# Two of four weight pieces of the sparse attention's compression in buffers outside the weight ring, and the keys of two branches in one tile

## Chip, cores and metric

The kernel runs on one core of a Trainium2 chip. The metric is the device time of one execution in microseconds; a time of the kernel is the median of its runs. Three runs of the kernel before took 1446.93, 1449.24 and 1449.49 us, so its time is 1449.24 us.

## What is computed

A decoder trunk of two layers on 512 tokens of width 1024, in float32. Each layer projects the normed input `h` through one matrix `w_in`, whose columns feed three token mixers that run side by side; their outputs are joined, projected through `w_out`, and a SwiGLU feed-forward block follows. The change lies in mixers A and B:

```python
h = rms_norm(x, norm_mix) * (1 + sc_m) + sh_m
(aq, ak, av, bq, bkc, bvc, bks, bvs, bkw, bvw, bg, cqkv, cz, ca, cb) = jnp.split(h @ w_in, points, axis=-1)
o_a = banded_attention(apply_rope(aq), apply_rope(ak), av, A_WINDOW, attn_sinks)
o_b = nsa_mixer(bq, bkc, bvc, bks, bvs, bkw, bvw, bg, ...)   # compressed, selected and window branches
o_c = gated_delta_net(cqkv, ca, cb, cz, ...)
x = x + gt_m * (jnp.concatenate([o_a, o_b, o_c], axis=-1) @ w_out)

def compress_tokens(x, w1, w2, pe):        # once for bkc, once for bvc
    win = concatenate([strides[:, :-1], strides[:, 1:]], axis=2) + pe   # 31 blocks of 32 tokens, stride 16
    return silu(win.reshape(31, 32 * 64) @ w1) @ w2                      # w1: 2048 x 256
```

## The kernel before, in words

Everything lies in SBUF, features on the 128 partitions. A projection of 128 columns of `w_in` takes a float32 weight piece, splits it into a high part `whi` (ScalarE, line 584) and a low part `wlo` (VectorE as a rule, line 585), and multiplies each of 8 slices in three matmuls of 128x512 (`product`, lines 588 to 595): 24 matmuls into a PSUM tile `pj`. The tiles `pj` of mixers A and B come from two PSUM banks in turn, so the third of them waits until the first has been read.

Weights come by DMA, all issued by one in-order queue, SP's. Each takes the next buffer of the **weight ring**, `wraw`: two buffers of 128x2048 floats (1 MB). An issue waits until the last reader of the buffer's former content is done: the split of a projection's piece, or the compression's matmuls.

Beside the ring there are buffers of 128x1024 floats, `ab0` to `ab3`. Through `ab0`, `ab1` and `ab2` goes in turn a side job of layer 0, `araw` (lines 385 to 445): pieces of the modulation weights `ada_w`, which ScalarE and GpSimd, at the end VectorE (line 416), sum up, and whose sum TensorE transposes (`pada`, line 438). Afterwards `aq` (queries of A), `bq` and `bqr` (queries of B, plain and rotated) live there.

The stage of the change is in `layer`, lines 987 to 1099, in this order:

- `single` on columns BKC, the inputs of the compression; `shifted` copies them into `kvx`;
- `single` on `raw2`, a second ring piece of 128 columns: the selected branch's keys (copied from the piece before, line 1063) and the window branch's keys (line 1064); `rope` rotates them into `ksw`;
- `squeeze(0)`; `single` on AK (line 1068), a ring piece of its own with the keys of mixer A, `rope_k`; `squeeze(1)`;
- `pair(AQ, rope_q)`: two projections with `squeeze(2)` and `squeeze(3)` behind them;
- the rest of the compression (`pct`, `pkc`, `pvc`), then `pair(BQ, both)`.

`squeeze(piece)` (lines 1044 to 1058) loads a quarter of the two compression weights `w1` as one ring tile `craw` (two DMAs of 512 KB), adds the position code to windows of `kvx` (`xw`, VectorE) and issues 8 small matmuls (32x256 results) into `pcmp`. The trace counts each float32 matmul of `pcmp`, `pi`, `psc`, `pt` twice.

A scheduler puts the recorded instructions of each engine into their final order; priorities (`prio`) shift some. So this stage is woven together with mixer C: a 64x64 inverse, whose first part is a ladder of 30 GpSimd operations (lines 844 to 848); VectorE takes its result at lines 850 to 853 (`td`), TensorE at 859 and 868 (`pi`), and so on to lines 893 to 906; then the recurrence over 4 chunks (`pvn`, `pks`, ...). Behind it come the attention blocks (`psc` scores, maxima `mx` at line 1133, softmax, `poa`, `pob`).

Of the kernel before, what the change touches and what calls it, by code (L numbers as in the profile page):

```python
# [8 lines left out]
F32 = mybir.dt.float32  # L9
# [9 lines left out]
NK = 8  # L19
# [23 lines left out]
 'cz0': 0,  # L43
 'czp': 0,
 'do': 1,
 'dtI': 'G',
 'e0': 'GGGV',
 'sv': 0,
# [126 lines left out]
  'wt': ['ab0', 'ab3', 'ab2', 'kvx']},  # L175
 {}]
KS[3].update({'sv': 4, 'ld': 1})
KN = {}


# [50 lines left out]
def trunk(ctx, tc, I, out, dbg=None):  # L231
    stage(0)
    nc = tc.nc
# [36 lines left out]
    AB3 = ("ab0", "ab1", "ab2")  # L270
    turns = {}

    def AB(name, shape=(128, 1024), dt=F32, tag=None, tags=AB3):
        if tag is None:
            turns[tags] = turns.get(tags, -1) + 1
            tag = tags[turns[tags] % len(tags)]
        pool = c8 if tag == "kvx" else ab
        t = pool.tile([128, 1024], dt, tag=tag, name=name)
        return t.rearrange("p (a b) -> p a b", a=shape[1]) if len(shape) == 3 else t
# [290 lines left out]
    def raw_piece(w, r0, nk, c0, n):  # L570
        raw = wr.tile([128, 2048], F32, tag="wraw", name="wraw")
        v = raw[:, :nk * n].rearrange("p (k c) -> p k c", k=nk)
        nc.sync.dma_start(v, w[r0:r0 + 128 * nk, c0:c0 + n].rearrange("(k p) c -> p k c", p=128))
        return v
# [54 lines left out]
    def layer(l, side, norm, vt):  # L629
# [100 lines left out]
        def pair(c0, then, first=None):  # L730
            raw = raw_piece(w_in, 0, NK, c0, 256) if first is None else first
            for j in range(2):
                to = j and first is not None and KN["sp"] >> l & 1
                to = [AB("wsp", (128, 8, 128), F32R, q) for q in ("ab3", "kvx")] if to else None
                with behind(l == 0 and c0 == CQKV + 768 and KN["ga"] & 1):
                    w = split(raw[:, :, j * 128:j * 128 + 128], to, E[KN["w0"]] if l == 0 and first is not None else V)
                p = P("mm" if first is None else "gd" if l else KN["cp"], "pj")
                for sl in HALF[2:] if first is None or (l == 0 and KN['fh']) else HALF[:2]:
                    product(p, w, h, 0, sl)
                then(p, j)  # L740
                with behind(l == 0 and first is not None and KN["ga"] & 2):
                    feed()
# [244 lines left out]
        def rope(p, dst):  # L987
            with prio("rope"):
                w = S2("sw")
                for r in range(4):  # L990
                    cpy(KN['ros'], w[32 * r:32 * r + 32], p[32 * (r ^ 1):32 * (r ^ 1) + 32])
                V.tensor_tensor(dst, p, const("cos"), op=OP.mult)
                E[KN["roM"]].tensor_tensor(w, w, const("sin"), op=OP.mult)
                V.tensor_add(dst, dst, w)
# [12 lines left out]
                for b in (slice(0, 64), slice(64, 128)):  # L1007
                    V.tensor_tensor(lo[b], src[a], hi[a].bitcast(F32), op=OP.subtract)

        aq, bq, bqr = (AB(n, (128, 2, 512), tag=t) for n, t in zip(("aq", "bq", "bqr"), AB3))  # L1010
        kvx = AB("kvx", (128, 2, 512), tag="kvx")
        ksw = c8.tile([128, 512], F32, tag="ksw", name="ksw")
        akd = AB("akd", (128, 2, 512), tag="ab3")
# [1 line left out]
        def single(view, then):  # L1015
            w = split(view)
            p = P("mm", "pj")
            product(p, w, h)
            then(p)
# [23 lines left out]

        def squeeze(piece):
            with prio("sq"):
                raw = wr.tile([128, 2, 4, 256], F32, tag="wraw", name="craw")
                for j, n in ((0, "cmp_k_w1"), (1, "cmp_v_w1")):
                    nc.sync.dma_start(raw[:, j], I[n][l, 512 * piece:512 * piece + 512].rearrange("(i p) c -> p i c", p=128))
                xw = xws[piece % 2]
                for j in range(2):  # L1050
                    win = bass.AP(tensor=kvx.tensor, offset=kvx.offset + 512 * j + 8 * piece,
                                  ap=[kvx.ap[0], [2, 4], [16, NCMP]])
                    V.tensor_tensor(xw[:, j, :, 0:NCMP], win,
                                    pet[:, 16 * j + 4 * piece:16 * j + 4 * piece + 4].unsqueeze(2).to_broadcast([128, 4, NCMP]),
                                    op=OP.add)
                    for i in range(4):
                        T.matmul(pc[32 * i:32 * i + 32, 256 * j:256 * j + 256], xw[:, j, i], raw[:, j, i],
                                 start=(piece == 0 and j == 0), stop=(piece == 3 and j == 1), tile_position=(0, 32 * i))

        raw = raw_piece(w_in, 0, NK, BKC, 256)  # L1060
        single(raw[:, :, 0:128], shifted)
        raw2 = wr.tile([128, 2048], F32, tag="wraw", name="wraw")[:, :1024].rearrange("p (k c) -> p k c", k=8)
        V.tensor_copy(raw2[:, :, 0:64], raw[:, :, 128:192])
        nc.sync.dma_start(raw2[:, :, 64:128], w_in[:, BKW:BKW + 64].rearrange("(k p) c -> p k c", p=128))
        single(raw2, lambda p: rope(p, ksw))

        squeeze(0)
        single(raw_piece(w_in, 0, NK, AK, 128), rope_k)
        squeeze(1)

        def rope_q(p, j):
# [23 lines left out]
        for hd in range(NH):  # L1095
            V.tensor_copy(vcb[32 * hd:32 * hd + NCMP, hd // 2, 64 * (hd % 2):64 * (hd % 2) + 64],
                          p[32 * hd:32 * hd + NCMP, 0:64])

        pair(BQ, both)
        if KN["czp"] == 2:  # L1100
            czs()
# [445 lines left out]
```

## Time and profile before

| | us |
|---|---|
| median of three runs | 1449.24 |
| profiled execution, its own time | 1450.83 |
| its span, first to last instruction | 1449.1 |
| TensorE busy | 1363.4 (94%) |
| VectorE busy | 975.1 (67%) |
| ScalarE busy | 685.9 (47%) |
| GpSimd busy | 496.9 (34%) |
| mean granted TensorE clock | 0.968 of 2.4 GHz |

Busy time of TensorE is modelled and does not mean full rate. The granted clock of a stretch is 1.00 at 2.4 GHz and 0.50 at 1.2 GHz. Of an idle time the profile names what ended it. Layer 0 reaches the stage of the change at about 185 us, layer 1 at about 890 us.

### The profile page before, as it was taken

What the parts mean: (1) busy time and instruction counts of PE and PEld (TensorE: products, weight loads), DVE (VectorE), ACT (ScalarE), POOL (GpSimd) and SP (SyncE); (2) the same over time, 40 slices, a digit from 0 to 9 for tenths busy, and PEclk for the clock granted to TensorE, in tenths of its full rate; (3) what the DMA queues carried; (4) which work ended last, traced back from release to release, by engine and by line L of the source; (5) the groups of instructions that cost most, each with busy time, mean ns of one, the idle gap of its engine ahead of it and who ended that gap; (6) DMA issues with size and microseconds to landing.
All of it is one profiled execution on the core that took longest, in us unless ns stands there. A gap on an engine that the chain in (4) does not pass through costs nothing.

```text
span 1449.1 us, 22839 instructions
## 1 busy us (share of the span) xinstructions
PE 1363.4 (94%) x8925; PEld 1166.2 (80%) x8925; DVE 975.1 (67%) x1773; ACT 685.9 (47%) x1250; POOL 496.9 (34%) x402
## 2 busy tenths in 40 slices
PE   3889988999999999999999999989989999999997
PEld 2667866877887888788898888667879999898997
DVE  6766886885646555456456667589647787777775
ACT  4576635574543432342245462568544444353441
POOL 4446541254432320140033013224335444253330
PEclk7799999799999999999999999989999999999999
DMA  9647453002147564555441123400130323323322
GB/s 325 208 159 231 142 173 124 29 2 88 30 146 244 162 204 140 166 174 174 133 146 34 59 88 103 153 30 2 43 104 16 121 97 99 106 94 110 117 88 74
DMA packets 137169, 171.57 MB, mean 118 GB/s; under 512 B 14779, under 2 KB 95333, under 8 KB 136933
## 3 DMA queue, kind: packets, MB, share of 16 engines
q1 hardware_dynamic: 137060, 170.11, 36.3%
q8 instruction: 70, 1.15, 0.3%
q14 instruction: 39, 0.31, 0.1%
HBM read 168.00 MB, written 2.10 MB: 117 GB/s over the span
## 4 chain that ended last, share of the span: by engine, by line
PE 66%; DVE 12%; DMA 7%; ACT 5%; POOL 4%; issue 4%; SPq 0%; POOLq 0%; DVEq 0%; ACTq 0%
PE pd L301 16%; PE pm L301 10%; PE pj L301 7%; PE pg L301 7%; PE pu L301 7%; DMA araw<-in_ada_w_dram 5%; PE pw L301 3%; PE psc L301 2%; DVE wlo L585 2%; POOL araw L421 2%; PE pwc L301 2%; PE ppt L1111 2%; PE pob L301 1%; PE pvt L301 1%; DVE araw L416 1%
## 5 line engine op out<-in xcount | busy, mean ns | idle before, releaser
L584 ACT ACTIVATE whi<-wraw 128x1024 fp32r<-128x1024 f32 (+1 forms) x181 | 179.3, 993 | 303.0 <-PE pd L301 99.2
L585 DVE TENSOR_TENSOR wlo<-wraw,whi 128x1024 fp32r<-128x1024 f32 (+1 forms) x171 | 218.5, 1279 | 107.1 <-ACT whi L584 104.9
L301 PE MATMUL pj<-hh,whi 128*128 128x512 f32 (+1 forms) x376 | 149.8, 400 | 7.1 <-DVE cacc L719 3.6
L301 PE MATMUL pj<-hl,whi 128*128 128x512 f32 (+1 forms) x376 | 147.9, 394 | 1.0 <-DVE hl L500 1.0
L301 PE MATMUL pj<-hh,wlo 128*128 128x512 f32 (+1 forms) x376 | 148.0, 394 | 0.8 <-DVE wlo L585 0.8
L421 POOL TENSOR_TENSOR araw<-araw 128x512 f32<-128x512 f32 x55 | 76.7, 1394 | 164.0 <-DMA araw<-in_ada_w_dram 62.8
L599 DVE SCALAR_TENSOR_TENSOR x<-pd,mods,x 128x512 f32<-128x512 f32 (+1 forms) x112 | 73.3, 671 | 65.2 <-PE pd L301 64.0
L301 PE MATMUL pd<-fl,whi 128*128 128x512 f32 x288 | 112.2, 390 | 0.0
L301 PE MATMUL pd<-fh,whi 128*128 128x512 f32 x288 | 111.1, 390 | 1.2 <-ACT whi L584 1.2
L301 PE MATMUL pd<-fh,wlo 128*128 128x512 f32 x288 | 107.3, 390 | 0.0
L301 PE MATMUL pm<-tmix,whi 128*128 128x256 f32 x576 | 102.8, 283 | 0.0
L301 PEld LDWEIGHTS pj<-hh,whi 128*128 128x128 f32 x376 | 72.6, 194 | 24.8 <-issue 5.5
L301 PEld LDWEIGHTS pm<-tmix,whi 128*128 128x128 f32 x576 | 88.2, 192 | 0.0
L301 PEld LDWEIGHTS pj<-hh,wlo 128*128 128x128 f32 x376 | 72.8, 194 | 16.6 <-DVE wlo L585 2.1
L301 PEld LDWEIGHTS pj<-hl,whi 128*128 128x128 f32 x376 | 73.1, 194 | 14.6 <-DVE hl L500 1.2
L301 PE MATMUL pg<-hh,whi 128*128 128x512 f32 (+1 forms) x208 | 78.2, 376 | 3.9 <-ACT hh L496 2.1
L301 PE MATMUL pg<-hh,wlo 128*128 128x512 f32 (+1 forms) x208 | 78.6, 378 | 2.2 <-DVE wlo L585 2.2
L301 PE MATMUL pu<-hh,wlo 128*128 128x512 f32 (+1 forms) x208 | 78.7, 378 | 1.8 <-DVE wlo L585 1.8
L421 POOL TENSOR_TENSOR araw<-araw,araw 128x512 f32<-128x512 f32 x36 | 51.3, 1426 | 81.5 <-ACT araw L420 80.3
L420 ACT ACTIVATE araw<-araw,scol 128x512 f32<-128x512 f32 x91 | 60.6, 715 | 39.1 <-DMA araw<-in_ada_w_dram 37.9
L301 PE MATMUL pg<-hl,whi 128*128 128x512 f32 (+1 forms) x208 | 78.0, 375 | 0.6 <-DVE hl L500 0.6
L301 PE MATMUL pu<-hl,whi 128*128 128x512 f32 (+1 forms) x208 | 77.9, 375 | 0.0
(383 smaller groups left out, 3646.0 us busy)
## 6 DMA issues: line engine op xcount, KB each, us to landing
wraw<-in_w_gate_up_dram SPq DMA_DIRECT2D x44, 1024.0 KB, 5.3
araw<-in_ada_w_dram SPq DMA_DIRECT2D x80, 512.0 KB, 3.9
wraw<-in_w_in_dram SPq DMA_DIRECT2D x22, 1024.0 KB, 5.1
wraw<-in_w_down_dram SPq DMA_DIRECT2D x20, 1024.0 KB, 5.3
araw<-in_ada_w_dram SPq DMA_DIRECT2D x8, 1024.0 KB, 8.3
wraw<-in_w_out_dram SPq DMA_DIRECT2D x8, 1024.0 KB, 5.1
craw<-in_cmp_k_w_dram SPq DMA_DIRECT2D x8, 512.0 KB, 4.0
craw<-in_cmp_v_w_dram SPq DMA_DIRECT2D x8, 512.0 KB, 4.9
```

The lines of the kernel that those rows point to most:

```text
L301: return T.matmul(o, l, r, start=start, stop=stop)
L416: V.scalar_tensor_tensor(o, t, scol[:, k:k + 1], acc, op0=OP.mult, op1=OP.add)
L420: A.activation(t, t, AF.Copy, scale=scol[:, k:k + 1])
L421: G.tensor_tensor(o, t, acc, op=OP.add)
L584: A.activation(hi, src, AF.Copy)
L585: eng.tensor_tensor(lo, src, hi.bitcast(F32), op=OP.subtract)
L599: V.scalar_tensor_tensor(xt[m][:, sl], p[:, sl], g, xt[m][:, sl], op0=OP.mult, op1=OP.add)
L1111: T.transpose(p[:, (o + kb) * 128:(o + kb) * 128 + 128], pt[:, kb * 128:kb * 128 + 128], ident)
```

## The change

Two edits. `squeeze` for pieces 0 and 2 (table entry `cab`) takes the buffers `ab1` (weights of the keys) and `ab2` (weights of the values) instead of a ring tile; pieces 1 and 3 stay in the ring. For that `bq` and `bqr`, which take the same buffers, are now named only ahead of `pair(BQ, both)`. And the columns AK are loaded into the unused half of the ring tile `raw2`, right behind the window keys, instead of into a ring tile of their own. The number of DMAs, their bytes and all arithmetic are the same.

```diff
--- before.py
+++ after.py
@@ -43,6 +43,7 @@
  'cz0': 0,
  'czp': 0,
  'do': 1,
+ 'cab': (0, 2),
  'dtI': 'G',
  'e0': 'GGGV',
  'sv': 0,
@@ -1007,7 +1009,7 @@
                 for b in (slice(0, 64), slice(64, 128)):
                     V.tensor_tensor(lo[b], src[a], hi[a].bitcast(F32), op=OP.subtract)
 
-        aq, bq, bqr = (AB(n, (128, 2, 512), tag=t) for n, t in zip(("aq", "bq", "bqr"), AB3))
+        aq = AB("aq", (128, 2, 512), tag="ab0")
         kvx = AB("kvx", (128, 2, 512), tag="kvx")
         ksw = c8.tile([128, 512], F32, tag="ksw", name="ksw")
         akd = AB("akd", (128, 2, 512), tag="ab3")
@@ -1043,9 +1045,13 @@
 
         def squeeze(piece):
             with prio("sq"):
-                raw = wr.tile([128, 2, 4, 256], F32, tag="wraw", name="craw")
+                if piece in KN["cab"]:
+                    raw = [AB("craw", tag=t).rearrange("p (a b) -> p a b", a=4) for t in AB3[1:]]
+                else:
+                    t = wr.tile([128, 2, 4, 256], F32, tag="wraw", name="craw")
+                    raw = [t[:, 0], t[:, 1]]
                 for j, n in ((0, "cmp_k_w1"), (1, "cmp_v_w1")):
-                    nc.sync.dma_start(raw[:, j], I[n][l, 512 * piece:512 * piece + 512].rearrange("(i p) c -> p i c", p=128))
+                    nc.sync.dma_start(raw[j], I[n][l, 512 * piece:512 * piece + 512].rearrange("(i p) c -> p i c", p=128))
                 xw = xws[piece % 2]
                 for j in range(2):
                     win = bass.AP(tensor=kvx.tensor, offset=kvx.offset + 512 * j + 8 * piece,
@@ -1054,18 +1060,19 @@
                                     pet[:, 16 * j + 4 * piece:16 * j + 4 * piece + 4].unsqueeze(2).to_broadcast([128, 4, NCMP]),
                                     op=OP.add)
                     for i in range(4):
-                        T.matmul(pc[32 * i:32 * i + 32, 256 * j:256 * j + 256], xw[:, j, i], raw[:, j, i],
+                        T.matmul(pc[32 * i:32 * i + 32, 256 * j:256 * j + 256], xw[:, j, i], raw[j][:, i],
                                  start=(piece == 0 and j == 0), stop=(piece == 3 and j == 1), tile_position=(0, 32 * i))
 
         raw = raw_piece(w_in, 0, NK, BKC, 256)
         single(raw[:, :, 0:128], shifted)
-        raw2 = wr.tile([128, 2048], F32, tag="wraw", name="wraw")[:, :1024].rearrange("p (k c) -> p k c", k=8)
+        raw2 = wr.tile([128, 2048], F32, tag="wraw", name="wraw").rearrange("p (k c) -> p k c", k=8)
         V.tensor_copy(raw2[:, :, 0:64], raw[:, :, 128:192])
         nc.sync.dma_start(raw2[:, :, 64:128], w_in[:, BKW:BKW + 64].rearrange("(k p) c -> p k c", p=128))
-        single(raw2, lambda p: rope(p, ksw))
+        nc.sync.dma_start(raw2[:, :, 128:256], w_in[:, AK:AK + 128].rearrange("(k p) c -> p k c", p=128))
+        single(raw2[:, :, 0:128], lambda p: rope(p, ksw))
 
         squeeze(0)
-        single(raw_piece(w_in, 0, NK, AK, 128), rope_k)
+        single(raw2[:, :, 128:256], rope_k)
         squeeze(1)
 
         def rope_q(p, j):
@@ -1096,6 +1103,7 @@
             V.tensor_copy(vcb[32 * hd:32 * hd + NCMP, hd // 2, 64 * (hd % 2):64 * (hd % 2) + 64],
                           p[32 * hd:32 * hd + NCMP, 0:64])
 
+        bq, bqr = (AB(n, (128, 2, 512), tag=t) for n, t in zip(("bq", "bqr"), AB3[1:]))
         pair(BQ, both)
         if KN["czp"] == 2:
             czs()
```

The scheduler orders the changed program anew. In the changed kernel the line numbers are higher, by 2 up to line 1043 of before and by 6 to 8 behind it (859 is 861, 1057 is 1063, 1133 is 1141).

SP's queue in layer 0, from the load of the window keys on (rows of 128x8x128 are AK, of 128x8x256 the two query tiles of A). Before:
```order
L1064 DMA wraw<-in_w_in_dram 128x8x64
L399 DMA araw_1306<-in_ada_w_dram 128x2x512
L399 DMA araw_1362<-in_ada_w_dram 128x2x512
L399 DMA araw_1366<-in_ada_w_dram 128x2x512
L1048 DMA craw<-in_cmp_k_w_dram 128x4x256
L1048 DMA craw<-in_cmp_v_w_dram 128x4x256
L399 DMA araw_1417<-in_ada_w_dram 128x2x512
L573 DMA wraw<-in_w_in_dram 128x8x128
L399 DMA araw_1413<-in_ada_w_dram 128x2x512
L1048 DMA craw<-in_cmp_k_w_dram 128x4x256
L1048 DMA craw<-in_cmp_v_w_dram 128x4x256
L573 DMA wraw<-in_w_in_dram 128x8x256
```
and in the changed kernel:
```order
L1070 DMA wraw<-in_w_in_dram 128x8x64
L401 DMA araw_1306<-in_ada_w_dram 128x2x512
L1071 DMA wraw<-in_w_in_dram 128x8x128
L401 DMA araw_1362<-in_ada_w_dram 128x2x512
L401 DMA araw_1366<-in_ada_w_dram 128x2x512
L1054 DMA craw<-in_cmp_k_w_dram 128x4x256
L1054 DMA craw<-in_cmp_v_w_dram 128x4x256
L401 DMA araw_1417<-in_ada_w_dram 128x2x512
L401 DMA araw_1413<-in_ada_w_dram 128x2x512
L1054 DMA craw<-in_cmp_v_w_dram 128x4x256
L575 DMA wraw<-in_w_in_dram 128x8x256
L1054 DMA craw<-in_cmp_k_w_dram 128x4x256 x2
```
AK is no longer behind two compression loads; what follows is piece 1 of the compression, then the value half of piece 0 and at once the queries of A. Before, these stood behind pieces 0 and 1.

VectorE in layer 0, behind the last sum of the side job (`kr`: keys of A being rotated; `lane`: the ladder's result, first step of the inverse on this engine; `wlo`: splits of the two query tiles of A). Before:
```order
L994 TENSOR_TENSOR ksw<-ksw,sw 128x512
L1053 TENSOR_TENSOR xw_102<-kvx,pet 128x4x31
L439 TENSOR_REDUCE mods_90<-pada 128x4
L1053 TENSOR_TENSOR xw_102<-kvx,pet 128x4x31
L440 TENSOR_TENSOR mods_90<-mods_90,vcol_88 128x4
L1053 TENSOR_TENSOR xw_103<-kvx,pet 128x4x31 x2
L992 TENSOR_TENSOR kr<-pj,cst 128x512
L993 TENSOR_TENSOR sw<-sw,cst 128x512
L585 TENSOR_TENSOR wlo<-wraw,whi 128x1024
L994 TENSOR_TENSOR kr<-kr,sw 128x512
L585 TENSOR_TENSOR wlo<-wraw,whi 128x1024
L850 TENSOR_SCALAR lane<-lane,cst 128x256 x2
```
and in the changed kernel:
```order
L995 TENSOR_TENSOR sw<-sw,cst 128x512
L587 TENSOR_TENSOR wlo<-wraw,whi 128x1024
L729 TENSOR_TENSOR cv<-pt,sg 128x4x128
L996 TENSOR_TENSOR ksw<-ksw,sw 128x512
L441 TENSOR_REDUCE mods_90<-pada 128x4
L442 TENSOR_TENSOR mods_90<-mods_90,vcol_88 128x4
L587 TENSOR_TENSOR wlo<-wraw,whi 128x1024
L994 TENSOR_TENSOR kr<-pj,cst 128x512
L995 TENSOR_TENSOR sw<-sw,cst 128x512
L996 TENSOR_TENSOR kr<-kr,sw 128x512
L1059 TENSOR_TENSOR xw_102<-kvx,pet 128x4x31 x2
L852 TENSOR_SCALAR lane<-lane,cst 128x256 x2
```
The two splits of the queries of A moved from right ahead of the ladder's result (`lane`) to ahead of the rotation of the keys of A.

TensorE in layer 0 at the first product of the inverse, `pi` of line 859 (861). Before:
```order
L301 MATMUL pj<-hh_278,whi 128x512
L301 MATMUL pj<-hl_279,whi 128x512
L301 MATMUL pj<-hh_278,wlo 128x512
L1057 MATMUL pcmp<-craw,xw_102 32x256
L859 MATMUL pi_1640<-td,at 32x32 x64
L1057 MATMUL pcmp<-craw,xw_102 32x256 x3
L301 MATMUL pj<-hh_276,wlo 128x512
```
and in the changed kernel:
```order
L303 MATMUL pj<-hl_279,whi 128x512
L303 MATMUL pj<-hh_278,wlo 128x512
L303 MATMUL pj<-hh_278,whi 128x512
L861 MATMUL pi_1640<-td,at 32x32 x64
L1063 MATMUL pcmp<-craw,xw_102 32x256 x8
L303 MATMUL pj<-hl_279,whi 128x512
L303 MATMUL pj<-hh_278,wlo 128x512
```
Between the last transposes of `cacc`, at 198.9 us in the trace, and this product there are 40 matmuls of `pj` and 21 of `pcmp` before, and 60 of `pj` and 16 of `pcmp` in the changed kernel.

## Rows read from the trace of the kernel before

**Rows 1.** Page, part 1: busy time of TensorE, its share, instructions.
```profile
PE 1363.4 (94%) x8925; PEld 1166.2 (80%) x8925; DVE 975.1 (67%) x1773; ACT 685.9 (47%) x1250; POOL 496.9 (34%) x402
```

**Rows 2.** Windows, layer 0: length, busy time of PE, PEld, DVE, ACT, POOL; clock, DMA share, GB/s.
```profile
203.20:207.00 3.80, 3.80 (x12) 2.97 (x11) 3.80 (x8) 0.00 (x0) 3.46 (x5) 0.55 0.68 214
...
213.90:217.10 3.20, 3.20 (x12) 2.55 (x9) 1.61 (x2) 2.51 (x4) 2.75 (x6) 0.50 0.25 16
...
253.60:268.00 14.40, 14.38 (x91) 11.71 (x92) 10.39 (x29) 4.88 (x13) 1.19 (x2) 0.50 0.19 71
```

**Rows 3.** Waits of TensorE, 190 to 270 us: total, times, longest, us.
```profile
PE psc L301 <- DVE mx L1133: 5.7, 1, 5.7
PE pj L301 <- ACT whi L584: 2.6, 1, 2.6
PE pada L438 <- DVE araw L416: 1.6, 1, 1.6
PE pcmp L1057 <- DMA craw<-in_cmp_k_w_dram: 0.7, 1, 0.7
```

**Rows 4.** Timeline of TensorE, layer 0: start, length (us), line, operation, tiles, count, wait before.
```profile
199.41 1.06 PE L1057 MATMUL pcmp<-craw,xw 128*32 128x256 f32 x12
...
204.40 0.63 PE L301 MATMUL pj<-hl,whi 128*128 128x512 f32 x1
...
206.11 0.63 PE L301 MATMUL pj<-hh,wlo 128*128 128x512 f32 x1
...
208.24 1.07 PE L1057 MATMUL pcmp<-craw,xw 128*32 128x256 f32 x16
...
221.67 1.29 PE L859 MATMUL pi<-td,at 32*32 32x32 f32 x128
...
223.78 0.39 PE L301 MATMUL pj<-hh,whi 128*128 128x512 f32 x1
...
228.34 0.39 PE L301 MATMUL pj<-hh,wlo 128*128 128x512 f32 x1
...
247.41 0.48 PE L301 MATMUL psc<-akd,aq 64*128 64x128 f32 x2
```

**Rows 5.** Timeline of SP's queue, layer 0: DMA issues.
```profile
196.90 0.37 SPq L1048 DMA_DIRECT2D craw<-in_cmp_k_w_dram  x1
...
203.33 0.37 SPq L573 DMA_DIRECT2D wraw<-in_w_in_dram  x1
...
223.57 0.37 SPq L573 DMA_DIRECT2D wraw<-in_w_in_dram  x1
```

**Rows 6.** Page, part 6: issues, KB each, median us to landing.
```profile
wraw<-in_w_in_dram SPq DMA_DIRECT2D x22, 1024.0 KB, 5.1
```

**Rows 7.** Timeline of ScalarE, layer 0.
```profile
228.78 2.00 ACT L584 ACTIVATE whi<-wraw 128x1024 fp32r<-128x1024 f32 x2 [5.17 <-DMA wraw<-in_w_in_dram]
...
240.78 2.39 ACT L305 ACTIVATE sw<-pj 32x512 f32<-32x512 f32 x4
```

**Rows 8.** Timeline of VectorE, layer 0.
```profile
195.66 1.21 DVE L585 TENSOR_TENSOR wlo<-wraw,whi 128x1024 fp32r<-128x1024 f32 x1
...
201.00 1.03 DVE L416 SCALAR_TENSOR_TENSOR araw<-araw,scol 128x512 f32<-128x512 f32 x1
...
217.67 0.61 DVE L850 TENSOR_SCALAR lane<-lane,cst 128x256 f32<-128x256 f32 x2 [2.17 <-POOL lane L848]
218.32 1.18 DVE L852 STREAM_TRANSPOSE td<-lane 128x512 f32<-128x512 f32 x1
```

**Rows 9.** Timeline of TensorE, layer 1.
```profile
909.47 0.50 PE L301 MATMUL pj<-hh,wlo 128*128 128x512 f32 x1 [0.52 <-DVE wlo L585]
...
916.04 0.50 PE L301 MATMUL pj<-hh,whi 128*128 128x512 f32 x1 [0.72 <-DVE kr L992]
```

**Rows 10.** Timeline of VectorE, layer 1.
```profile
914.77 0.61 DVE L850 TENSOR_SCALAR lane<-lane,cst 128x256 f32<-128x256 f32 x2 [3.86 <-POOL lane L848]
915.30 0.68 DVE L992 TENSOR_TENSOR kr<-pj,cst 128x512 f32<-128x512 f32 x1
```

## Prediction

> **What bounds the kernel.** Three views, in this order. The page first: TensorE is busy for 1363.4 us [rows 1] of a span of 1449.1, so a change in one stage is worth what TensorE idles there, and what it loses at the low clock. Then the waits of TensorE around the stage [rows 3]: 1.6 us for the side job's last sum, 2.6 for the split of the first query tile of A, 0.7 for a compression load, together 4.9; and, after the last projection, 5.7 for the maxima of the scores. Then the windows behind them [rows 2]: 3.8 us at 0.55 and 3.2 us at 0.50 of the clock. At half rate half the time is lost, so 1.7 + 1.6 = 3.3 us. The stage itself wastes 4.9 + 3.3 = 8.2 us in layer 0, and after the wait for scores 14.4 us pass at 0.50.
>
> SP's queue tells why. The queries of A are issued at 203.33, behind both compression pieces, when the matmuls of piece 0 have given back a ring buffer [rows 5]. A load of this kind lands after 5.1 us [rows 6], so at 208.4. TensorE has then just finished the keys of A: at 208.24 it turns to compression matmuls [rows 4], and then it has nothing.
>
> **The change, step by step, layer 0.** The ring has to pass six pieces in this stage instead of nine; bytes and matmuls stay the same.
>
> *The load of the queries.* Its buffer is now `raw2`, free when the keys of A are split: 195.66 + 1.21 = 196.9 [rows 8]. Ahead of it on SP stands only the value half of piece 0, whose buffer a VectorE sum ahead of that split frees. So it is issued 6.4 us earlier and lands at 202.0. Behind it on SP wait the key half of piece 0 (free only with `pada`, 202.7), then pieces 3 and 2; the key half lands about 5 us later, by 208, and is needed at 210. On VectorE the two splits of the queries now stand ahead of the key rotation, two cheap copies for the modulation and the ladder's result. If they had to wait for the load, these would wait too; with the load at 202.0 and 1.0 us for the high part, the input is there at 203.0, and they run at once.
>
> *TensorE up to the first product of the inverse.* Twenty projection matmuls take 223.78 to 228.34, so 0.228 us each; eight of `pcmp` take 1.0 [rows 4]. The new order has 60 projections (13.7 us), 16 `pcmp` (2.0) and the transposes of `pada` (0.6) from 199.41 on. Two waits remain: `pada` comes up at 201.3 and its sum ends at 201.00 + 1.03 [rows 8], so 0.7; the low part of a tile is late by 0.5, as now in layer 1 [rows 9]. With 0.3 for changes between tiles TensorE arrives at 217.2. But the product needs `td`, and line 850 starts at 217.67 only because the GpSimd ladder ends then; line 852 ends at 218.32 + 1.18 = 219.5 [rows 8], one small window addition now in between makes it 219.9. Nothing ahead of the ladder is changed. So **a new wait of 2.7 us** stands here, and the product starts at 219.9 instead of 221.67 [rows 4]. That is 1.8 us earlier, and with 20 projections more (4.6) and 5 `pcmp` less (0.6) behind it: 5.8 us ahead.
>
> *The clock.* The waits of 1.6 and 2.6 us were each followed by the low clock, the 0.7 alone cannot be told apart [rows 2, 3]. I charge the new wait with 1.6, the smaller of the two losses: 4.2 us ahead. The Trainium skill (TensorE: Matmul & The Clock Gate, "What's actually happening") calls the half rate the default state and says that activity releases it. The two stretches agree: they end while dense projections run. What that rule would do where thin work follows the wait is a rival below; by it the gain would be gone.
>
> A second count, by waits alone: removed 8.2; new 0.7 + 0.5 + 2.7 + 1.6 = 5.5; gain 2.7. The two differ by gaps too small to be named as waits. I take the first, which goes by places, and keep 2.7 as the lower bound.
>
> *The scores behind the stage.* They wait for VectorE's queue, which starts with the rotation of B's first query tile; ScalarE begins that at 240.78 [rows 7]. In the new order this tile has moved up: 219.9 + 1.2 for the product + 2.0 for 16 `pcmp` + 2.5 for 11 projections + 1.2 for the second product + 1.0 for `pct` + 3.4 for 15 projections + 1.6 for the clock = 232.8, and 1.6 for a split and a copy ahead of the rotation: 234.4, 6.4 us earlier. So VectorE gains 6.4 where TensorE gains 4.2, and the wait of 5.7 shrinks by up to 2.2. This asks for the load of B's queries in time. It waits for the matmuls of piece 1, about 212, behind piece 2: with 5.1 us for each, 222.4, needed at 223.6. Now it is issued at 223.57, and the split waits 5.17 for it [rows 5, 7]. I take 5.3, between 4.2 and 6.4.
>
> *Layer 1.* Waits of 0.52 and 0.72 [rows 9]. The second is for the bank that the key rotation reads (line 992, at 915.30), and this stands on VectorE behind the ladder's result (914.77) in both orders [rows 10]. TensorE comes earlier to the same gate and waits longer. Bounds: a gain of 1.2 when both waits really go; a loss of 1.6 when the gathered wait lowers the clock as in layer 0. I take a loss of 0.5, nearer to the second, since the gate does not move.
>
> *The rest.* In both attentions the same instructions are woven in another order. No row prices that. I take 0 and allow 2.6 either way, the longest wait seen inside the stage. Loading piece 0 of layer 1 much earlier, and the wider stride of the split's source, cost nothing that TensorE waits for.
>
> **Sum.** 5.3 - 0.5 = 4.8 us. The profiled execution took 1450.83, so 1446.0; the median of the three runs is 1.6 lower, so **1444.4 us**.
>
> **The rivals.**
>
> *Given back (same).* The ladder is the real bound: TensorE gains 1.8 at the product, and the changed order of the attention and the clock take the rest. For it: the ladder does not move, and in layer 1 it gates already. Against it: behind the product the load of B's queries is early as well. By the lower bound of 2.7 less the 0.5 and a further 0.7: 1.5 us, 1447.7.
>
> *Clock (slower).* The two gathered waits, 2.7 us in layer 0 and about 2 in layer 1, are followed by the thin work of the inverse and `pcmp`, not by dense projections. Where little ran, after the 5.7 wait, the clock stayed at 0.50 for 14.4 us [rows 2]. At the low clock a projection takes (206.11 - 204.40) / 4 = 0.43 [rows 4], 0.2 more. I have charged 8 of them. With 32 the gain of 4.8 is gone; it is slower by over 0.2% from 46 on, and with 50 it gives 1444.4 + 8.4 = 1452.8. Against it: in the present order thin work stands at the same places, without a wait ahead of it, and the low clock ended after 3 to 4 us.
>
> *Much faster.* The waits go as worked out, the clock does not fall at the product, and the wait of 5.7 with half of its 14.4 us at low clock shrinks further: about 4 more, 1440.
>
> *The load stays late.* If the queries of A landed at 208.4 as now, TensorE would idle 5 us from 204 on and reach the product at about 222: no change, 1449. It speaks against this that nothing on SP ahead of that load waits for longer than 196.9; its chance is in that of the first rival.
>
> **How the numbers follow.** About 0.2%, 2.9 us, can be told from no change. Forecast 0.56; given back, with the late load, 0.22; much faster 0.10; clock 0.12. The forecast with its own bounds reaches from 1441.5 to 1447; all but 0.02 of it lies below 1446.3. So faster 0.54 + 0.10 = 0.64, same 0.02 + 0.22 = 0.24, slower 0.12. The range takes in the given-back case with its 2.6 us of attention, leaves out most of the clock case and the far end of the much faster one: 1438.5 to 1451.
>
> **What would show it.** In the changed kernel's profile: the issue of the queries of A at about 197 and no wait of TensorE for their high part; one wait of 2 to 3 us ahead of the first `pi`, which starts at about 220; low clock for some 3 us behind it; B's query rotation on ScalarE at 234 to 235; the scores' wait near 3.5 us. In layer 1 the first `pi` at an unchanged distance from the ladder. I am wrong if the queries' load is still issued after 200, if `pi` starts after 221.5, or if the windows behind it show the low clock for over 8 us.

## Result, and the profile of the changed kernel

Seven runs of the changed kernel took 1436.08 to 1443.84 us, median 1439.41; seven of the kernel before 1446.93 to 1453.24, median 1449.24. The ratio is 0.9942, 95% interval 0.9925 to 0.9959: 8.4 us faster, between 5.9 and 10.9 (the two medians lie 9.8 apart). A second measurement (run e5 below) gave 0.9946 (0.9925 to 0.9968). The prediction was 1444.4, range 1438.5 to 1451: the right side, inside the range but close to its lower end, and 5 us too high (3.6 by the ratio).

The profiled execution of the changed kernel took 1443.84 us. It was already 2.35 us ahead when layer 0's stage began, with the same instructions up to there: the last transposes of `cacc` start at 196.54 and not at 198.89. To compare places in layer 0 with before, add 2.35 to its times.

The page, part 1, answers to [rows 1]:

```profile
PE 1361.6 (94%) x8925; PEld 1167.6 (81%) x8925; DVE 968.1 (67%) x1773; ACT 687.5 (48%) x1250; POOL 496.8 (34%) x402
```

TensorE is busy for 1.8 us less (before: 1363.4) in a span that is 7.1 us shorter: most of what went is idle time. The waits of TensorE, 188 to 268 us, answer to [rows 3]:

```profile
PE psc L303 <- DVE mx L1141: 3.8, 2, 3.2
PE pi L861 <- DVE td L854: 2.2, 1, 2.2
PE pada L440 <- DVE araw L418: 0.8, 1, 0.8
PE pj L303 <- DVE wlo L587: 0.8, 1, 0.8
```

The wait of 2.6 for the high part of A's queries and the 0.7 for a compression load are gone, the one for the side job is 0.8 instead of 1.6, the one for the scores 3.2 instead of 5.7. New are 2.2 for `td`, the ladder's result, and 0.8 for a low part. The waits inside the stage thus sum to 3.8 us, before to 4.9: by waits alone the stage has won little. SP's queue in layer 0, against [rows 5] (first row the queries of A, last row those of B, between them the compression):

```profile
194.56 0.37 SPq L575 DMA_DIRECT2D wraw<-in_w_in_dram  x1
200.46 6.28 SPq L1054 DMA_DIRECT2D craw<-in_cmp_k_w_dram  x2
...
210.26 0.37 SPq L575 DMA_DIRECT2D wraw<-in_w_in_dram  x1
```

The queries of A are issued at 194.56 + 2.35 = 196.9 (before: 203.33), those of B at 212.6 (223.57). ScalarE, against [rows 7]: the first split of B's queries and the rotation of B's first tile:

```profile
219.25 1.06 ACT L586 ACTIVATE whi<-wraw 128x1024 fp32r<-128x1024 f32 x1 [5.58 <-DMA wraw<-in_w_in_dram]
...
232.43 1.79 ACT L307 ACTIVATE sw<-pj 32x512 f32<-32x512 f32 x3
```

VectorE takes the ladder's result, against [rows 8]:

```profile
215.59 0.62 DVE L852 TENSOR_SCALAR lane<-lane,cst 128x256 f32<-128x256 f32 x2 [5.83 <-POOL lane L850]
...
216.39 1.05 DVE L854 STREAM_TRANSPOSE td<-lane 128x512 f32<-128x512 f32 x1
```

TensorE at the first product, at the first scores and at the end of the longest wait for their maxima, against [rows 4]:

```profile
217.59 1.44 PE L861 MATMUL pi<-td,at 32*32 32x32 f32 x128 [2.19 <-DVE td L854]
...
239.19 0.48 PE L303 MATMUL psc<-akd,aq 64*128 64x128 f32 x2
...
245.08 0.58 PE L303 MATMUL psc<-akd,aq 64*128 64x128 f32 x1 [3.20 <-DVE mx L1141]
```

Before, that wait ended here:

```profile
253.59 0.79 PE L301 MATMUL psc<-akd,aq 64*128 64x128 f32 x2 [5.70 <-DVE mx L1133]
```

The product starts 4.08 us earlier than before, 1.73 without the offset; the scores 8.22, or 5.87; the wait ends 8.51 earlier, or 6.16. The first scores are a little flattered: 92 small `pi` products of the inverse (as the trace counts them), which stood ahead of them, now stand behind them, where TensorE waits anyway. The windows of the two stretches at the low clock, and of the one behind the product in layer 1 (columns as in [rows 2]):

```profile
217.60:222.00 4.40, 4.40 (x150) 2.42 (x151) 4.20 (x7) 1.34 (x2) 0.42 (x1) 0.61 0.03 10
242.40:259.40 17.00, 14.31 (x91) 12.09 (x92) 14.03 (x39) 8.25 (x23) 2.34 (x3) 0.50 0.17 63
910.50:915.00 4.50, 3.70 (x133) 3.33 (x134) 1.82 (x3) 3.20 (x6) 0.51 (x1) 0.62 0.02 4
```

**Where the time went.** Six instructions with the same operands in every kernel bound four stretches of TensorE's queue: in each layer the stage (from the last `pt<-cst,cacc`) and the attention (up to the first matmul `pg` or `pu` of the feed-forward block). The stage ends at the first `psc` in layer 0 and at the last `pj` in layer 1. So the wait for the first maxima, 5.7 us before, counts to the attention of layer 0. For layer 1, before:

```profile
900.40 0.38 PE L726 MATMUL pt<-cst,cacc 128*128 128x128 f32 x2
...
943.53 0.39 PE L301 MATMUL pj<-hh,wlo 128*128 128x512 f32 x1
...
1083.04 0.39 PE L301 MATMUL pg<-hh,whi 128*128 128x256 f32 x1 [2.11 <-ACT hh L496]
```

and after:

```profile
894.16 0.38 PE L728 MATMUL pt<-cst,cacc 128*128 128x128 f32 x2
...
937.99 0.40 PE L303 MATMUL pj<-hh,wlo 128*128 128x512 f32 x1
...
1074.78 0.39 PE L303 MATMUL pg<-hh,whi 128*128 128x256 f32 x1 [2.09 <-ACT hh L498]
```

So the stage of layer 1 is 0.70 longer (43.83 against 43.13) and its attention 2.72 shorter (136.79 against 139.51). In layer 0 the stage is 5.87 shorter, the attention 1.25. Together -9.14; with the offset of -2.35, +3.23 in the feed-forward block of layer 0, whose instructions are the same in almost the same order, and +1.33 behind layer 1's attention, that makes the 6.9 us by which TensorE ends earlier in this execution. The 3.23 is not the change's: the repeat of the same kernel (e5) has -0.32 there. It is the clock, which was at half rate at the start of that block in this execution, so 3.4 us lost, and not in e5:

```profile
378.92:385.75 6.83, 6.44 (x31) 6.35 (x31) 3.91 (x9) 3.08 (x8) 3.98 (x5) 0.50 0.02 4
```
```profile
374.20:385.00 10.80, 9.86 (x79) 9.60 (x80) 9.87 (x22) 7.95 (x20) 5.72 (x8) 1.00 0.01 2
```

### The profile page after: what moved, and what is told of

Its sections match the earlier page's. It is cut to its first block, busy times and chain, and to the rows that moved or that the text cites. A ratio compares the mean times of both kernels' runs of the same rounds, so it can differ in the third digit from the quotient of the medians.

```text
span 1442.0 us, 22848 instructions
## 1 busy us (share of the span) xinstructions
PE 1361.6 (94%) x8925; PEld 1167.6 (81%) x8925; DVE 968.1 (67%) x1773; ACT 687.5 (48%) x1250; POOL 496.8 (34%) x402
## 4 chain that ended last, share of the span: by engine, by line
PE 65%; DVE 12%; DMA 8%; POOL 6%; issue 4%; ACT 4%; SPq 0%; POOLq 0%; DVEq 0%; ACTq 0%
PE pd L303 15%; PE pm L303 10%; PE pu L303 7%; PE pg L303 7%; DMA araw<-in_ada_w_dram 7%; PE pj L303 6%; POOL araw L423 3%; PE pwc L303 3%; PE pw L303 3%; DVE wlo L587 2%; PE psc L303 2%; PE pob L303 2%; PE ppt L1119 2%; DVE araw L418 1%; POOL lane L850 1%
```

## The experiments

Each has six to twelve runs, beside runs of the kernel before on the same chip (medians 1447.98 us for e1 to e4, 1446.48 for e5 to e8, 1445.97 for e9 to e12; so ratios are compared, not medians). The table gives for each the median, the ratio to before with its interval, and from its one profile the start of the first product (from the last `cacc`) and the four stretches, all as differences to before in us.

| run | median | ratio (95%) | product L0 | stage L0 | attention L0 | stage L1 | attention L1 |
|---|---|---|---|---|---|---|---|
| the change, first | 1439.41 | 0.9942 (0.9925-0.9959) | -1.73 | -5.87 | -1.25 | +0.70 | -2.72 |
| e5, the change again | 1441.10 | 0.9946 (0.9925-0.9968) | -1.73 | -7.64 | -1.35 | +0.62 | -2.74 |
| e1, keys of A merged only | 1448.45 | 1.0002 (0.9988-1.0017) | -0.85 | -0.81 | +0.09 | -0.25 | +0.22 |
| e2, buffers only | 1444.80 | 0.9975 (0.9959-0.9991) | -2.85 | -3.08 | -1.98 | +0.79 | -1.96 |
| e3, layer 0 only | 1441.43 | 0.9955 (0.9940-0.9970) | -1.74 | -6.14 | -0.39 | -0.34 | -0.62 |
| e4, layer 1 only | 1449.93 | 1.0017 (1.0002-1.0033) | -0.46 | -0.42 | -0.85 | +0.72 | +0.03 |
| e6, selection on GpSimd, changed | 1447.80 | 1.0003 (0.9987-1.0019) | -2.68 | -4.75 | -0.65 | +3.53 | -2.52 |
| e7, the same, before | 1449.82 | 1.0016 (0.9997-1.0034) | +1.06 | +1.06 | 0.00 | +0.46 | -0.04 |
| e8, piece 0 only | 1455.94 | 1.0056 (1.0037-1.0076) | -1.75 | -3.73 | +5.58 | +0.79 | +0.44 |
| e9, ladder's last 3 steps on VectorE | 1439.40 | 0.9950 (0.9930-0.9969) | -2.06 | -7.98 | -1.22 | +0.82 | -2.65 |
| e10, last 4 steps | 1449.67 | 1.0030 (1.0016-1.0045) | -2.02 | -5.28 | +4.93 | +0.72 | +0.25 |
| e11, ladder longer | 1453.32 | 1.0052 (1.0032-1.0072) | -1.14 | -6.20 | +5.36 | +0.78 | +0.44 |
| e12, before, ladder longer | 1449.58 | 1.0024 (1.0008-1.0041) | +0.53 | -0.73 | +0.18 | -0.40 | +0.78 |

A single profile holds about 1 us of chance in a stretch (layer 0 of e4 and e12 has the instructions of before but for a few, and shows -0.85 to +0.18); its feed-forward blocks more, by the clock just shown. The one profile of before is also of an execution that is longer than most (1450.83, against medians of 1446 to 1449): in all but one of the others the stage of layer 0 begins 0.6 to 4.3 us earlier. So totals are read from the ratios and places from the profiles.

**e1, the merged keys alone.**

```diff
- 'cab': (0, 2),
+ 'cab': (),
```

> Only the second edit: the keys of A share the tile of the window keys; all four compression pieces stay in the weight ring. Theory (early loads): the queries of A still follow pieces 0 and 1 in the ring, so their load waits for the matmuls of piece 0 and is issued at 200 us or later, the waits for it stay, and the time is 1447 to 1450 us, within 0.2% of before. Rival (new order of the attention): any re-ordering of the program loosens the attention, so that this one too is 4 us or more faster than before.

Measured: no difference. The queries of A are issued at 202.74 and the wait for their high part is still there, 2.6:

```profile
202.74 0.37 SPq L575 DMA_DIRECT2D wraw<-in_w_in_dram  x1
```
```profile
PE pj L303 <- ACT whi L586: 2.6, 1, 2.6
```

The theory holds. The rival is not tested by it: TensorE's instructions have the order of before, so the merge alone re-orders nothing there.

**e2, the buffers alone.**

```diff
-        single(raw2[:, :, 128:256], rope_k)
+        single(raw_piece(w_in, 0, NK, AK, 128), rope_k)
```

> Only the first edit: compression pieces 0 and 2 in the idle buffers, the keys of A again in a ring piece of their own. Theory (early loads): the queries of A follow the keys of A in that ring buffer and are issued when these are split, about 197 us as in the full change; B's queries early too. So nearly all of the gain: 1439 to 1443 us. Rival (both edits are needed, since the ring passes a piece more and piece 1 or 3 comes late): a wait of TensorE for a compression load of 2 us or more appears, 1444 to 1447 us.

Measured: 3.6 us faster (1.3 to 5.9), under half of the full change. The load of A's queries is early (issued at 194.53), yet the stage gains only 3.08: the order differs, and TensorE waits 2.8 for `td` and 2.7 for a later step of the inverse. No wait for a compression load appears, so neither theory has it right, though the time lies in the rival's range: both loads are early, as in the full change. That the order behind them makes the difference is likely, but no run separates it from the ring's extra piece.

**e3 and e4, one layer at a time.**

```diff
 KS[3].update({'sv': 4, 'ld': 1})
+KS[0]['cab'] = (0, 2)
```

with `'cab': ()` in the table and the merged keys in that layer alone (e4: `KS[2]`, layer 1).

> Both edits in layer 0 alone, layer 1 as before. Theory (the prediction): all of the gain is made in layer 0, so the time equals that of the full change or is 0.5 us lower: 1439 to 1440 us. Rival (layer 1 gains as well, since in its trace the distance to before grows by about 1.7 us behind its first projections): 1441 to 1443 us.

> Both edits in layer 1 alone, layer 0 as before. Theory (the prediction): the ladder gates the first product of the inverse in both orders, so nothing or a loss of 0.5 us: 1449 to 1450 us. Rival (layer 1 gains as well): 1445.5 to 1447.5 us, with one or both waits of 0.5 and 0.7 us gone and the first product earlier against the ladder.

Measured: layer 0 alone 6.5 us faster (4.3 to 8.7), layer 1 alone 2.5 slower (0.3 to 4.8). In the traces layer 0 gains 6.1 in its stage, and the stage of layer 1 loses 0.7, in e4 as in the full change. The theory of e4 has the sign of layer 1 right, and its 0.5 lies within the interval; e3 lies in the rival's range, though layer 1 gains nothing by itself. The parts sum to 4.0 us, not 8. Part of the rest is in the last column: the full change has 2.7 us less in layer 1's attention, e4 nothing. The instructions there are the same. Their order is not: in e4 it is, but for a few places, that of before, in the full change another. The order of layer 1 depends on what the scheduler did in layer 0: even e3, whose layer 1 has the code of before, has another order in its attention.

**e5, the full change again.** No edit.

> The full change once more, beside the others. By the parts measured alone (layer 0: 6.5 us faster, layer 1: 2.0 us slower, medians of 12 runs) the sum is 4.5 us: 1443 to 1444 us. Rival (the first seven runs, 8.4 us faster, hold, so that the two layers help each other): 1439 to 1441 us.

Measured: 7.8 us faster (4.6 to 10.8) than the runs of before beside it, median 1441.10 (the medians lie 5.4 apart). The intervals of the two measurements of the full change overlap almost wholly. The sum of the parts, 4.0, has an interval of about 0.9 to 7.1 (an estimate from the two), so the times alone do not show that the layers depend on each other. The profiles do: the 2.7 us of layer 1's attention come back in e5 (2.74), and neither e3 nor e4 has them.

**e6 and e7, an earlier ladder.** Two steps on VectorE select the ladder's operand; in layer 0 other work stands between them.

```diff
-            V.scalar_tensor_tensor(a16, al[:, :, 16:32], m1, a16, op0=OP.mult, op1=OP.add)
+            G.tensor_scalar(pr, al[:, :, 16:32], m1, None, op0=OP.mult)
+            G.tensor_tensor(a16, a16, pr, op=OP.add)
```

> The full change, and the selection ahead of the ladder partly on GpSimd (a product and a sum there in place of VectorE's second step), which lets the ladder of layer 0 start about 2 us earlier; in layer 1, where VectorE does both steps at once, it starts about 0.5 us later, but the key rotation is ordered ahead of the ladder's result. Theory (the ladder gates TensorE in the changed kernel): the wait ahead of the first product becomes shorter or the product starts about 2 us earlier in layer 0, and in layer 1 the wait for the key rotation goes: 1 to 4 us faster than the full change. Rival (the wait at the ladder costs nothing, since what comes behind is bound by other work): within 1 us of the full change.

> The same edit of the selection on the kernel before. Theory (before, TensorE comes to the first product later than the ladder's result, being short of weights): the earlier ladder gives nothing in layer 0 and costs up to 0.5 us in layer 1: 1447.5 to 1449 us, within 0.2% of before. Rival (the ladder binds before as well): 2 us or more faster.

Measured: e6 gives the whole gain back, e7 is 2.3 us slower (interval from 0.4 faster to 4.9 slower). In e6 the first product does come earlier (2.68 against 1.73), but the scores do not (4.75 against 5.87), and the wait for their maxima is the old one.

```profile
PE psc L303 <- DVE mx L1142: 5.7, 1, 5.7
PE pi L862 <- DVE td L855: 2.1, 1, 2.1
```

And in layer 1, where the key rotation now stands ahead of the ladder's result and no longer keeps TensorE waiting, it waits elsewhere, and the stage is 3.53 longer. Its waits there, 884 to 940 us, the longest of them without a cause that the profile names:

```profile
PE pj L303 <- issue: 2.5, 1, 2.5
PE pi L862 <- DVE td L855: 1.5, 1, 1.5
PE pi L871 <- DVE pq L865: 0.8, 1, 0.8
```

Both theories of e6 fall; the edit moves more than the ladder. In e7 the product stands behind two more projections (0.5 us) and a longer wait for the side job (2.1 instead of 1.6), and comes 1.06 later: the earlier ladder bought nothing there, as its theory says.

**e8, only piece 0 outside the ring.**

```diff
- 'cab': (0, 2),
+ 'cab': (0,),
```

> Both edits, but only piece 0 in the idle buffers; piece 2 stays in the ring. The queries of A are still loaded early, but the load of B's queries now waits for the matmuls of piece 2 and not of piece 1. Theory (both loads count, A's for about 4 us at the first product, B's for the rest): the wait of ScalarE for B's queries stays at 5 us or more and TensorE waits for them: 1444 to 1446 us. Rival (only the queries of A count): as the full change in the same call, within 1 us.

Measured: 8.1 us slower than before (5.4 to 11.0). Both theories fail. B's queries are issued later than in the full change (213.44 against 210.26), but they are split at 218.78 and not later: the loads are as early as in the full change, and the first product too (-1.75). The scores come 3.73 earlier. All of it and more goes in the attention of layer 0, 5.58 us longer. (The four stretches make 3.1 of the 8.1 us; 3.65 more stand in the feed-forward block of layer 0 of this profile.) The longest waits of TensorE in e8, 247 to 387 us:

```profile
PE pob L303 <- ACT ptt L307: 3.6, 4, 1.4
PE ppt L1119 <- DVE sc L1159: 1.6, 2, 1.1
...
PE pw L303 <- DVE lsum L1220: 1.3, 1, 1.3
PE poa L303 <- ACT ptt L307: 1.1, 1, 1.1
```

Softmax weights (`ptt`, `sc`, `lsum`) come late for the products that this order has put next; the waits for maxima are gone. In all TensorE idles 12.9 us in this stretch, before 8.7.

**e9 to e11, the ladder at a fixed order, and the order at a nearly fixed ladder.** In e9 and e10 layer 0 takes its last three (`j >= 12`) or four (`j >= 11`) ladder steps on VectorE:

```diff
+                e = V if l == 0 and j >= 12 else G
-                G.tensor_tensor(pr[:, :n], a16[:, j + 1:, j:j + 1].to_broadcast([128, n, 16]),
+                e.tensor_tensor(pr[:, :n], a16[:, j + 1:, j:j + 1].to_broadcast([128, n, 16]),
```

and in e11 GpSimd has two more operations behind the ladder:

```diff
+            for _ in range(2 if l == 0 else 0):
+                G.tensor_tensor(xl[:, 15:], xl[:, 15:], pr[:, :1], op=OP.mult)
```

> The full change, with the last three of the 15 steps of layer 0's ladder on VectorE instead of GpSimd (1.9 us there). TensorE, ScalarE and SP keep the order of the full change. Theory (the ladder gates the first product of the inverse): the steps are shorter on VectorE, the wait ahead of the product shrinks from 2.2 us by 0.2 to 0.8, and the time is up to 1 us lower than that of the full change: ratio to before 0.993 to 0.995. Rival (the wait costs nothing, as work behind it is bound elsewhere): the first scores start no earlier.

> As e9, with the last four steps. The ladder ends a little earlier still, but now the scheduler weaves the attention of both layers in another order than in the full change. Theory of the prediction (the loads and the ladder decide, the order of the attention costs 0 with 2.6 us either way): 0.5 to 1 us faster than the full change, ratio 0.993 to 0.994. Rival (some 3 to 4 us of the full change's gain come from its order of the attention, above all in layer 1): 2 to 5 us slower than the full change, ratio 0.996 to 0.998.

> The full change with two more GpSimd multiplications behind layer 0's ladder (0.3 us each; the last row of its result is multiplied twice more). The order of TensorE is that of e10 but for two instructions, so a ladder longer by 0.6 us than in the full change, and by more than 1 us than in e10, at the same order of the attention. Theory of the prediction: 0.6 us slower than the full change and about 1.3 us slower than e10. Rival (the order of the attention): 3 to 6 us slower than the full change, again with most of it behind the stage.

e9 keeps the order of TensorE, ScalarE and SP. Its wait ahead of the product is 1.8 instead of 2.2; product and scores start 0.33 and 0.34 earlier than in e5: in this order the ladder is the gate, and what it gives is passed on. The median cannot show half a microsecond (0.9950 against 0.9946); e9 is no better version by measurement.

e10 has TensorE's order of the full change up to about the first product and in the stage of layer 1, and another one behind that product and in both attentions, whose instructions are the same. The product comes as early as in the full change or earlier (-2.02), and the kernel is slower than before. Against the full change the attention is 6 us longer in layer 0 and 3 in layer 1. e11 has a longer ladder (product 0.9 later than in e10) at that same order but for two instructions, and nearly the same stretches. So the rival holds, and more strongly than it was put: with another order the kernel goes from 0.5% faster to 0.3% slower, 11.6 us from e9 to e10, of which the profiles have 9.1 in the two attentions and 2.7 in layer 0's stage.

Where: the attention of layer 0 in the changed kernel, in e10, and in e10 the part at the low clock (in the changed kernel the window 242.40 to 259.40 above):

```profile
239.19:377.65 138.46, 132.05 (x1026) 109.41 (x1023) 97.14 (x306) 83.32 (x224) 58.02 (x47) 0.94 0.12 39
```
```profile
239.98:384.62 144.64, 134.46 (x931) 108.56 (x930) 101.11 (x307) 83.55 (x224) 58.29 (x47) 0.92 0.11 37
242.43:266.32 23.89, 19.80 (x105) 14.47 (x106) 16.65 (x47) 10.92 (x30) 4.02 (x5) 0.50 0.13 45
```

TensorE idles (length less busy time) 10.2 us of the stretch and not 6.4, and it is busy at half rate for 19.8 us and not 14.3, which costs 2.7 more. Together 6.5, about the 6.2 by which the stretch is longer (an estimate from these rows). Of the idle time, waits for the scores' maxima make 5.9, against 3.8 in the changed kernel:

```profile
PE psc L303 <- DVE mx L1142: 5.9, 3, 4.5
```

On VectorE the first maximum stands 4.6 us behind the first scores (at 244.62), with two steps of the stacking of the selected keys (`bks`) between; in the changed kernel 1.9 us behind them (at 241.04).

**e12, a longer ladder before the change.** The same two lines as in e11, with 8.

> The kernel before with eight more GpSimd multiplications behind layer 0's ladder (about 2.5 us; the last row of its result is multiplied eight times more); the order of the other engines stays but for two places. Theory (before the change the ladder's result lies ready 2.2 us before TensorE comes to the first product): the product is 0 to 0.5 us later, the time within 0.2% of before. Rival (the ladder binds before the change as well): 2 to 2.5 us slower, with a wait for the ladder's result ahead of the product.

```profile
222.61 1.28 PE L861 MATMUL pi<-td,at 32*32 32x32 f32 x128 [0.33 <-DVE td L854]
```

VectorE takes the ladder's result 2.6 us later than before. The wait is 0.33, the product 0.53 later, with three projections and three compression matmuls more ahead of it; the end of the stage is not later at all. So the ladder had 2.2 us to spare before the change, as read from [rows 4, 8]; after it, none. The median is 3.5 us above before (1.2 to 5.9), which the theory did not expect. In the profile it lies in the feed-forward block of layer 0, 2.89 us longer there. The clock was at half rate at its start for 6.83 us, as in the changed kernel's first profile and in that of e1, whose time is that of before. Whether it falls there more often with the longer ladder, one profile does not settle.

## Why the prediction was right, and where it fell short

- **The load of the queries.** Predicted: issue at 196.9, 6.4 earlier. Measured: 196.9, with the offset. e1 shows that without it there is no gain.
- **The first product.** Predicted: a new wait of 2.7, the product at 219.9, 1.8 earlier. Measured: 2.19, and 219.94, 1.73 earlier, the same in e5 and e3. TensorE came 0.5 later to the gate than worked out (waits of 0.8 and 0.8 ahead of it, not 0.7 and 0.5), and the gate decided, as forecast. e12 and e9 confirm that it changed hands from the load to the ladder.
- **The clock behind it.** Predicted: a loss of 1.6. In the profiled execution 4.4 us at 0.61, so 1.7 lost; in e5, the same program with the same wait, none, and the stage is 1.77 us shorter. The term is right in size and present in some executions only.
- **Two counts.** The prediction's count by waits comes out to the digit: 8.2 removed, 0.8 + 0.8 + 2.2 + 1.7 = 5.5 new, a gain of 2.7. Yet the places gained 5.87 and more. The prediction took the count by places, and that was the better one; what lies between the two, beyond the `pi` products that moved, no row names.
- **Scores.** Predicted: B's rotation at 234.4, B's queries landed at 222.4, a wait near 3.5, TensorE 4.2 ahead at the first scores and up to 6.4 behind the wait, so 5.3. Measured: 234.8, split at 221.6, 3.2, 5.87 ahead at the first scores (6.14 in e3; 7.64 in e5, where the clock did not fall) and 6.16 behind the wait.
- **Layer 1.** Predicted: a loss of 0.5, since the gate does not move. Measured: 0.62 to 0.82 in every kernel with the new order in layer 1's stage and the ladder there as it was. The waits are 1.2 and 0.9 instead of 0.5, 0.2 and 0.7, and the product stands 2.96 behind the ladder's end (before 3.21); the window behind it shows 4.5 us at 0.62, so 1.7 lost.
- **The attention: the step that failed.** "No row prices that. I take 0 and allow 2.6 either way." Measured: in layer 1 -2.72, in the repeat -2.74, which alone is more than the allowance for both; in layer 0, from the end of the wait for the scores on, -0.96 and -1.06. The four stretches gained 9.1 us where the sum has 4.8, and 3.7 of the 4.3 between them are this term. And e8, e10 and e11 show that the attention of layer 0 can as well cost 4.9 to 5.6. The longest wait inside the stage was no bound for it: the re-ordering moves several waits at once, and the low clock with them.

In layer 1 the 2.7 us are waits, above all for maxima and softmax weights. Before, 943 to 1083 us:

```profile
PE psc L301 <- DVE mx L1133: 2.5, 5, 0.9
PE pi L301 <- DVE lane L893: 2.2, 1, 2.2
PE pob L301 <- ACT ptt L305: 1.8, 2, 1.5
PE psc L301 <- DVE cs L1200: 0.7, 1, 0.7
```

and after, 937 to 1075 us:

```profile
PE pi L303 <- DVE lane L895: 2.1, 1, 2.1
PE psc L303 <- DVE mx L1141: 1.6, 2, 1.1
PE pvn L303 <- DVE cv L947: 0.5, 1, 0.5
PE pob L303 <- ACT ptt L307: 0.2, 1, 0.2
```

Without the wait of the inverse for `lane`, which stays, that is 5.0 before and 2.3 after: the 2.7. Of the rivals, *clock* and *given back* did not come; the time fell at the value of *much faster*, but only a part of its reason is there: the clock did not fall in e5, and the remaining gain is the attention's. Nearly the same edit with another order, e10, is 0.3% slower than before, by which the forecast "faster" would have failed; there the attention takes back what the stage gains, which is what *given back* was about. The prediction had the mechanism of the stage. That the order of the attention then added to the gain and did not take it back was luck.

## What to carry to other kernels

A load made earlier is worth the distance to the next gate: here the product gained 1.7 of the 6.4 us, the rest came because the next load was early too. Where a scheduler orders the whole program anew, an edit is measured together with a new order of everything behind it: look there for waits before crediting the edit, and make two or three near-identical edits that are ordered differently, to learn what the order is worth (here some 9 us in the attentions, more than the edit). No run has the full change's order of the attention without its edits; that the order would give its share there too is not shown.

## What was not expected of the hardware

**The same wait, two clocks.** Behind the wait of 2.2 us for `td` the granted clock fell in the first execution (window above, 0.61) and not in e5, the same program:

```profile
216.00:220.40 4.40, 4.38 (x164) 2.77 (x165) 4.33 (x8) 2.62 (x3) 0.45 (x1) 1.00 0.04 10
```

It fell in e3 as well, and not in e9, where the wait was 1.8. The Trainium skill (TensorE: Matmul & The Clock Gate, "What's actually happening") says that the number of slow matmuls at the start of the same kernel varies between runs; these two executions vary likewise, in the middle of a kernel. A term for the clock behind a short wait is a chance, not a price.

**GpSimd's ladder is slowed by VectorE.** In the kernel before, layer 1, a step of 96 columns takes 1.32 us while VectorE splits a weight piece, and the next narrower one, without it, 0.33 (in layer 0 of the same profile, 96 columns without a split take 0.36):

```profile
908.31 1.32 POOL L846 TENSOR_TENSOR lane<-lane 128x96 f32<-128x96 f32 x1
909.71 1.46 POOL L848 TENSOR_TENSOR lane<-lane 128x96 f32<-128x96 f32 x1
911.25 0.33 POOL L846 TENSOR_TENSOR lane<-lane 128x80 f32<-128x80 f32 x1
```
```profile
908.19 1.23 DVE L585 TENSOR_TENSOR wlo<-wraw,whi 128x1024 fp32r<-128x1024 f32 x1 [0.20 <-ACT whi L584]
...
909.71 1.20 DVE L585 TENSOR_TENSOR wlo<-wraw,whi 128x1024 fp32r<-128x1024 f32 x1
```

Each of the two splits lengthens the ladder by about 1 us. The Trainium skill (SBUF — State Buffer, "SBUF: two separate sides") has this as an exclusive port: of a VectorE operation with two SBUF inputs and a GpSimd operation that reads SBUF, the one that starts first blocks the other for its whole length; the rows agree.

**An earlier issue that lands no earlier.** B's queries, issued at 210.26 behind other loads, were split 9.0 us later (the prediction had 10.2, 5.1 for each of two loads); in e8, issued at 213.44, 5.3 us later. The DMA engines moved 242 and 243 GB/s between 205 and 218 us in the two, so the same bytes in that time.
